# Where the modulation of both layers and the scan's step sizes run in a two-layer hybrid diffusion block

## The chip, the cores and the metric

The kernel runs on one core of a Trainium2 chip, as one program. The time is that of a whole execution on the device, in microseconds (us), median of repeated runs. The core has five engines with instruction streams of their own, each in order: TensorE (PE) for matmuls, VectorE (DVE), ScalarE (ACT), GpSimd (POOL), and SyncE (SP), which here only issues DMAs. They wait for each other by semaphores.

## What is computed

Two layers act on 1024 latent and 256 context tokens, 1024 wide, fp32. A conditioning vector for the latent tokens, another for the context, gives by a 1024 x 6144 product per layer shifts, scales and gates (the *modulation*), 12 columns of 512:

```python
x = rms_norm(...); h = modulate(x, shift, scale)      # h * (1 + scale) + shift
p = h @ w_in                                          # split into three head groups:
#  A  6 heads of latent attention (low-rank q and kv, rotary key), all keys
#  B  6 heads of bidirectional Mamba-2 scan: conv, SiLU, then
dt = softplus(dt_raw + dt_bias)                       # step sizes, (tokens, 2 directions, 6 heads)
da = -exp(a_log) * dt                                 # decays, summed within chunks of 128 tokens
#  C  4 heads of attention in a window of +-128 tokens, with a sink logit
x = x + gate * (concat(A, B, C) @ w_out)
x = x + gate * convglu(modulate(rms_norm(x)))         # w_up, conv, gate, w_down
```

Context tokens see only context tokens; in layer 2 their output is not needed. The output is a final RMSNorm of the latent tokens.

## The kernel before, in words

Activations lie feature by token. A large product is split into high and low parts and done as three PE passes (`hhi*wh`, `hlo*wh`, `hhi*wl`), so a weight tile takes ACT a rounding (`wh`) and DVE a subtraction (`wl`, L424) before PE can use it.

A layer runs thus. `w_in_ssd` (L634) projects `krdt` (rotary key and raw step sizes) and the gate z, rotates the key (`kr_rope`, L704, with DVE's L790 to L793), then makes seven columns of scan inputs `xbc`, each with a conv on DVE (L508), stored to `fmd` and, transposed, to `tmd`: the *scan columns*. Then the attention projections, with the scan (`ssd`, L803) and after it the window attention (`swa`) as side work, then six heads of latent attention. `mix` (L1494) splits the eight mixed row blocks into high and low parts; `w_out` multiplies; `ffn` has an up part with a conv and a down part (FFN-down).

PE's order is that in which the code emits it. Background generators are stepped by a model clock: each `yield g` says that its next piece comes g model us later, and `bg` (with a delay), `tick`, `drain` and `until` work through them between the foreground's matmuls. Nothing else moves a background matmul on PE. The other engines' orders come from a scheduler with priorities, and are in order when they run.

The modulation is done in two ways. `mods` (L301) gives it to PE: the conditioning is the stationary operand, four column groups at once, in two halves of 1 MB of weights a column; `mod_out` (L364) copies the result (L368), transposes it and sums. `mods_v` (L329) gives it to DVE: multiply-accumulates with the conditioning as a scalar (L352, L354), for one or two *streams* (latent, context), then transposes on PE and sums (L361). In layer 1, columns 10 and 11 go by `mods`, 4 to 9 by `mods_v`, both in the background of the scan columns. Layer 2's 12 columns go by `mods_v` in the background of layer 1's FFN-down, the first four with two streams.

In `ssd` the step sizes (from `krdt`, transposed: `pdt`), decays and their sums (`pacs`, `pacT`) come first, then the chunks of the scan. `last` (L2022), at the start of the last attention head, splits five of the eight blocks, numbers 4 and 1 with POOL; 6 and 7 follow when the side work ends, and 2 in `w_out`. The output weights are loaded once the window attention has been emitted.

Of the kernel before, what the change touches and what calls it, by code (L numbers as in the profile page):

```python
# [9 lines left out]
F32 = mybir.dt.float32  # L10
# [49 lines left out]
def _rope_tables():  # L60
# [21 lines left out]


PACE = {
    'dt': (22.0, 22.0),
    'back0': (4.0, 4.0),
    'back': (3.0, 3.0),
    'cb': (0.5, 0.5),
# [26 lines left out]
class Emit:  # L115
# [187 lines left out]
    def mods(self, l, ns, wtile, ahead, gap, etile=None):  # L303

        nc, I = self.nc, self.I
        if len(self.modT) == l:
            self.modT.append(self.C.tile([128, 6, 2, 8], F32, name=f"modT{l}"))
        todo = [(n, half) for n in ns for half in range(2)]
        ready = []

        def load():
            if todo:
                n, half = todo.pop(0)
                ws = []
                for kp in (2 * half, 2 * half + 1):
                    w = wtile([128, 2, 512])
                    self.last_w = nc.sync.dma_start(out=w, in_=I['w_mod'][l, kp * 256:(kp + 1) * 256, n * 512:(n + 1) * 512]
                                                    .rearrange("(k p) n -> p k n", p=128))
                    ws.append(w)
                ready.append(ws)  # L320

        if ahead:
            load()
        for n in ns:
            pm = None
            for half in range(2):
                load()
                yield gap
                ws = ready.pop(0)  # L329
                pm = pm or self.b("pm")  # L330
                for i in range(4):
                    self.mm(out=pm[32 * i:32 * i + 32, :], lhsT=self.st[:, half * 4 + i, :], rhs=ws[i // 2][:, i % 2, :],
                            start=(half == 0), stop=(half == 1))
            yield from self.mod_out(l, n, pm, etile or wtile)
# [465 lines left out]
        return h, lo  # L800


    def ssd(self, l, krdt, out):  # L803
        nc, c = self.nc, l == 0
        sm = self.small[l]
        es = ExitStack()
        M = PoolTags(es.enter_context(self.tc.tile_pool(name=f"M{l}", bufs=1, reuse_waits="tile")),
                     {"small": 1, "fm": 2, "tm": 3, "ab": 4, "L": 3, "xw": 2, "cb": 2, "hf": 2, "hb": 2, "z": 2, "t": 1})
        S_ = M.tile([128, 4, 120], F32, tag="small", name=self.nm("sml"))
        dt, bias_, etot, wst = [S_[:, i, :] for i in range(4)]  # L810
        S2 = self.u(shape=[128, 10, 128], name="sml2")
        dta, tot, de, t1, av, t2 = [S2[:, i, 0:120] for i in range(6)]
        acs = de
        aexp, aT = S2[:, 6, 0:12], S2[0:120, 7, :]
        triF, triB = S2[:, 8, :], S2[:, 9, :]
        self.tri(triF, 0)
        self.tri(triB, 1)
        c3 = lambda ap: ap.rearrange("p (c j) -> p c j", j=12)
# [29 lines left out]
        nc.vector.tensor_copy(c3(acs)[:, :, 0:6], c3(p1[:, 0:120])[:, :, 0:6])  # L848
        nc.vector.tensor_copy(c3(acs)[:, :, 6:12], c3(p1[:, 120:240])[:, :, 6:12])
        nc.vector.tensor_copy(tot, p1[:, 240:360])  # L850
        yield 2.0
        p2 = self.b("pacT")
        self.tr(p2[:120, 0:128], acs)
        nc.vector.tensor_copy(aT, p2[:120, 0:128])
# [7 lines left out]
        nc.scalar.activation(etot, tot, AF.Exp)  # L862
        nc.vector.tensor_mul(wst, de, dt)

        yield 2.0

        def load_tm(k):
            t = M.tile([128, 5, 128], F32, tag="tm", name=self.nm("tm"))
# [26 lines left out]
        xw = weigh(tms[0], order[0], 1)  # L895
# [484 lines left out]
    def mla_att(self, l, vt, kbuf, qh, load, maxes, Y, last):  # L1380
# [37 lines left out]
        for h in range(NH):  # L1418
            if h % 2 == 0:
                Y[h // 2] = self.u(name="ya")  # L1420
            if h == NH - 1:
                last()
            mx = maxes(h + 1) if h + 1 < NH else iter(())
            acc = self.W.tile([128, SEQ], F32, tag="wlo", name=self.nm("acc"))
            py = self.f("py")
# [9 lines left out]
            for kt in range(NCH):  # L1435
# [19 lines left out]
                next(mx, None)  # L1455
                if kt == 2 and h + 2 < NH:
                    load(h + 2)
                self.tick()
            if c:
                Pc = ctx_scores(h, terms)  # L1460
# [492 lines left out]
    def body(self):  # L1953
# [17 lines left out]
        for l in range(DEPTH):  # L1971
# [10 lines left out]
            with ExitStack() as es:  # L1982
                self.TD = PoolTags(es.enter_context(tc.tile_pool(name=f"TD{l}", bufs=1, reuse_waits="tile")), {"t": 2, "tt": 2, "wm": 6})
                if c:
                    def early():
                        wt = lambda shape, name="wm": self.TD.tile(shape, F32, tag="wm", name=self.nm(name))
                        prm = self.load_params(1, wt)
                        next(prm)
                        yield from self.mods(0, (10, 11), wt, True, 3.0)
                        next(prm, None)  # L1990
                        yield from self.mods_v(0, range(4, 10), wt, 3.7, lag=6.0)
                    self.bg(early())
                next(w_in)
                self.drain()

# [1 line left out]

            def side():
                self.scan = True
                yield from self.ssd(l, krdt, out)  # L2000
                self.scan = False
                self.bg(self.scan_norm(l, Y, out["vst"]), PACE['sn0'][l])
                yield from self.swa(l, Y)
# [6 lines left out]
                while not self.ready:  # L2010
                    yield 2.0
                for i in (6, 7):
                    self.mix(l, Y, i, hl, i in (4, 1))

            self.ready, self.paced = False, True
            self.bg(side())
# [2 lines left out]
            kbuf, qh, load, maxes = self.mla_loads(l)  # L2019
            vt = self.mla_proj(l, kva, qn, kbuf, qh, load, maxes)  # L2020

            def last():  # L2022
                self.ready = True
                for i in (3, 4, 5, 0, 1):
                    self.mix(l, Y, i, hl, i in (4, 1))

            finish = self.mla_att(l, vt, kbuf, qh, load, maxes, Y, last)
            self.drain()
# [6 lines left out]
            if l + 1 < DEPTH:  # L2035
# [7 lines left out]
                    return self.X.tile(shape, F32, tag="wm", name=self.nm("wm"))  # L2043

                def mods():
                    yield from self.mods_v(l + 1, range(12), xw, 3.8, xa, lambda n: 2 if n < 4 else 1, lag=5.0)
                    self.gated = True

                self.gated = False
                nxt = Norm(self, x, l + 1, 0, CHUNKS, CHUNKS[:2])  # L2050
                self.ffn(l, x, norm, nxt.feed, lambda: self.bg(mods(), 14.0), lambda: self.until(lambda: self.gated))
                h, need = (nxt.hi, nxt.lo), nxt.need
            else:
                feed = self.final(x)
# [182 lines left out]
```

## Time and profile before

| | us |
|---|---|
| three runs | 3250.32, 3252.76, 3253.66 (median 3252.76) |
| profiled execution | 3254.55 |
| its span on the core | 3252.8 |
| PE busy | 3052.2 (94%) |
| DVE busy | 2124.4 (65%) |
| ACT busy | 1273.7 (39%) |
| POOL busy | 597.1 (18%) |

The span counts from the first to the last instruction of the core. PE rows have modelled ends: consecutive full-width products start 0.23 us apart at the full clock, though each is shown as 0.39 long. A stretch with PE below 100% is one in which it waits.

### The profile page before, as it was taken

How to read it: one execution, taken by the hardware profiler on the slowest of the kernel's cores; microseconds unless marked ns; L12 is line 12 of the kernel's file. 1: busy time of each engine (PE TensorE's matmuls, PEld its weight loads, DVE VectorE, ACT ScalarE, POOL GpSimd, SP SyncE). 2: the span in 40 equal slices, each digit the busy share in tenths (PEclk: the TensorE clock that was granted, in tenths of full speed). 3: DMA queues.
4: the chain of work that ended last, by engine and by line, in shares of the span. 5: the costliest groups of instructions: out<-in, count | busy, mean ns of one | idle time of the engine just before them, and what ended most of it. 6: DMA issues, size and time to landing. Idle time of an engine off the chain costs nothing.

```text
span 3252.8 us, 40148 instructions
## 1 busy us (share of the span) xinstructions
PE 3052.2 (94%) x15369; PEld 2400.3 (74%) x15369; DVE 2124.4 (65%) x3134; ACT 1273.7 (39%) x2204; POOL 597.1 (18%) x375
## 2 busy tenths in 40 slices
PE   7989978998999999998999999888999999999998
PEld 4778754554878888887888788754557778888887
DVE  4784887776285665658875734788563677677544
ACT  5333543444163343443111533553342454444212
POOL 2104533443100000000000303544452000000001
PEclk9989988999999999999999999988999999999999
DMA  8765675202302212227543345655113122225321
GB/s 270 219 192 140 215 230 165 48 16 81 110 30 72 78 62 72 68 68 288 176 155 95 124 117 171 209 185 145 42 39 110 52 78 82 88 83 181 130 75 62
DMA packets 349247, 392.41 MB, mean 121 GB/s; under 512 B 37202, under 2 KB 276451, under 8 KB 349056
## 3 DMA queue, kind: packets, MB, share of 16 engines
q1 hardware_dynamic: 348092, 389.62, 38.0%
q8 instruction: 121, 1.98, 0.3%
q0 software_dynamic: 704, 0.14, 0.1%
q14 instruction: 70, 0.57, 0.1%
q10 hardware_dynamic: 260, 0.10, 0.0%
HBM read 284.48 MB, written 104.01 MB: 119 GB/s over the span
## 4 chain that ended last, share of the span: by engine, by line
PE 79%; DVE 13%; DMA 3%; ACT 2%; issue 2%; POOL 1%; SPq 0%; DVEq 0%; ACTq 0%; POOLq 0%
PE p L143 36%; PE X L143 10%; PE Z L143 7%; PE s L143 5%; PE py L143 5%; PE pc L143 4%; PE V L143 3%; PE Y L143 3%; DVE mx L1358 1%; PE pm L143 1%; PE pn L143 1%; DVE wm L354 1%; PE pst L143 1%; DMA xr<-in_x_dram 1%; DVE sh L791 1%
## 5 line engine op out<-in xcount | busy, mean ns | idle before, releaser
L143 PE MATMUL p<-gh,wb 128*128 128x512 f32 (+1 forms) x1760 | 504.9, 370 | 0.0
L436 ACT CAST wb<-w 128x512 fp32r<-128x512 f32 (+1 forms) x412 | 251.6, 613 | 599.8 <-PE p L143 308.8
L437 DVE TENSOR_TENSOR wb<-w,wb 128x512 fp32r<-128x512 f32 (+1 forms) x412 | 279.5, 680 | 237.8 <-ACT wb L436 236.6
L143 PEld LDWEIGHTS p<-gh,wb 128*128 128x128 f32 x1760 | 321.0, 189 | 55.9 <-issue 0.2
L1568 DVE SCALAR_TENSOR_TENSOR x<-p,modT,x 128x512 f32<-128x512 f32 (+1 forms) x280 | 193.5, 695 | 254.0 <-PE p L143 253.7
L143 PE MATMUL X<-hb,wb 128*128 128x512 f32 x1440 | 340.4, 389 | 1.6 <-DVE cm L1606 1.6
L143 PE MATMUL p<-gl,wb 128*128 128x512 f32 (+1 forms) x880 | 325.3, 370 | 0.3 <-DVE gl L1747 0.3
L143 PEld LDWEIGHTS X<-hb,wb 128*128 128x128 f32 x1440 | 270.1, 188 | 58.5 <-DVE cm L1606 2.5
L143 PE MATMUL p<-hhi,wh 128*128 128x512 f32 (+1 forms) x792 | 293.4, 378 | 5.5 <-ACT z L643 3.2
L143 PE MATMUL p<-hlo,wh 128*128 128x512 f32 (+3 forms) x792 | 291.3, 369 | 1.4 <-POOL hlo L2139 0.9
L143 PE MATMUL p<-hhi,wl 128*128 128x512 f32 (+1 forms) x744 | 273.5, 368 | 3.0 <-DVE wl L424 2.3
L143 PE MATMUL Z<-hb,wb 128*128 128x512 f32 x960 | 231.4, 390 | 3.8 <-ACT cm L1608 3.8
L1442 ACT ACTIVATE P<-s 128x512 f32<-128x512 f32 x240 | 142.5, 598 | 231.6 <-PE s L143 221.0
L2085 POOL TENSOR_TENSOR acc<-acc,sq 128x512 f32<-128x512 f32 x24 | 32.1, 1340 | 1024.0 <-ACT sq L2084 1024.0
L143 PEld LDWEIGHTS Z<-hb,wb 128*128 128x128 f32 x960 | 178.8, 188 | 40.9 <-ACT cm L1608 4.6
L1449 POOL TENSOR_TENSOR acc<-acc,P 128x1024 f32<-128x1024 f32 x69 | 169.5, 2457 | 197.9 <-ACT P L1442 171.8
L143 PEld LDWEIGHTS p<-gl,wb 128*128 128x128 f32 x880 | 166.7, 189 | 28.3 <-DVE gl L1747 0.8
L143 PEld LDWEIGHTS p<-hhi,wh 128*128 128x128 f32 x792 | 152.7, 194 | 34.8 <-issue 4.4
L143 PE MATMUL py<-P,vt 128*64 128x512 f32 (+3 forms) x744 | 174.5, 585 | 0.0
L143 PEld LDWEIGHTS p<-hlo,wh 128*128 128x128 f32 (+1 forms) x792 | 150.6, 190 | 25.0 <-DVE hlo L2133 1.5
L143 PEld LDWEIGHTS p<-hhi,wl 128*128 128x128 f32 x744 | 143.2, 193 | 27.4 <-DVE wl L424 3.2
L354 DVE SCALAR_TENSOR_TENSOR wm<-wm,mstat,wm 128x512 f32<-128x512 f32 x196 | 141.1, 745 | 19.9 <-DMA wm<-in_w_mod_dram 19.2
(406 smaller groups left out, 5952.9 us busy)
## 6 DMA issues: line engine op xcount, KB each, us to landing
wm<-in_w_mod_dram SPq DMA_DIRECT2D x96, 512.0 KB
w<-in_ffn_w_up_dram SPq DMA_DIRECT2D x88, 512.0 KB
w<-in_ffn_w_down_dram SPq DMA_DIRECT2D x32, 512.0 KB
w<-in_w_in_dram SPq DMA_DIRECT2D x30, 512.0 KB
gd<-ft SPq DMA_DIRECT2D x22, 640.0 KB
gr<-gd SPq DMA_DIRECT2D x22, 640.0 KB
ab<-acsd SPq DMA_DIRECT2D x36, 384.0 KB
tm<-tmd SPq DMA_DIRECT2D x38, 320.0 KB
```

What stands on the lines that cost most here:

```text
L143: self.nc.tensor.matmul(out=out, lhsT=lhsT, rhs=rhs, start=start, stop=stop, **kw)
L354: nc.vector.scalar_tensor_tensor(out=acc[:, v, :], in0=w[:, i, :], scalar=c, in1=acc[:, v, :], op0=ALU.mult, op1=ALU.add)
L436: self.nc.scalar.copy(t[:, 0], raw)
L437: self.nc.vector.tensor_sub(t[:, 1], raw, t[:, 0])
L791: nc.vector.tensor_mul(sh[:rows, LAT], sh[:rows, LAT], sin[:rows, LAT])
L1358: nc.vector.tensor_reduce(out=m[:, j, s:s + 1], in_=p, axis=AXX, op=ALU.max)
L1442: nc.scalar.activation(P[:, q * 512:(q + 1) * 512], s, AF.Exp, scale=sc)
L1449: (nc.vector if kt in ((2, 4, 6, 8) if self.scan else (4, 7)) else nc.gpsimd).tensor_add(acc, acc, P)
L1568: self.nc.vector.scalar_tensor_tensor(out=t[:, s:e], in0=p[:, 0:e - s], scalar=self.mcol(l, v, m)[:, o:o + 1], in1=t[:, s:e], op0=ALU.mult ...
L2085: (nc.gpsimd if self.n[ch] < 6 else nc.vector).tensor_add(acc, acc, sq[:, :n])
```

## The change

Layer 1's modulation columns 4 to 11 all go to PE, in one call, with the transposes of layer 2's parameters (`prm`) behind them. Layer 2's first four columns go to PE too, and start 8 instead of 14 model us into FFN-down; the other eight stay on DVE. The first part of `ssd` becomes `ssd_dt`, a background generator of its own in the scan columns, with new model times. `last` is in two parts, the second in the middle of the last head, and no `mix` uses POOL.

```diff
 PACE = {
-    'dt': (22.0, 22.0),
+    'dt': (40.0, 16.0),
+    'dt2': (12.0, 8.0),
...
     def mods(self, l, ns, wtile, ahead, gap, etile=None):
...
             self.modT.append(self.C.tile([128, 6, 2, 8], F32, name=f"modT{l}"))
+            nc.vector.memset(self.modT[l], 0.0)
...
-    def ssd(self, l, krdt, out):
+    def ssd_dt(self, l, krdt, out):
...
-        S_ = M.tile([128, 4, 120], F32, tag="small", name=self.nm("sml"))
-        dt, bias_, etot, wst = [S_[:, i, :] for i in range(4)]
-        S2 = self.u(shape=[128, 10, 128], name="sml2")
+        S_ = self.u(shape=[128, 10, 128], name="sml")
+        dt, bias_, etot, wst, dta, tot, de, t1, av, t2 = [S_[:, i, 0:120] for i in range(10)]
+        out["dt"] = dt, bias_, etot, wst
+        S2 = self.u(shape=[128, 4, 128], name="sml2")
...
         nc.vector.tensor_copy(tot, p1[:, 240:360])
-        yield 2.0
+        yield PACE['dt2'][l]
...
         nc.vector.tensor_mul(wst, de, dt)
-        yield 2.0
+    def ssd(self, l, out):
...
+        dt, bias_, etot, wst = out["dt"]
...
             if h == NH - 1:
-                last()
+                last(0)
...
+                if kt == 4 and h == NH - 1:
+                    last(1)
...
-                        yield from self.mods(0, (10, 11), wt, True, 3.0)
+                        yield from self.mods(0, range(4, 12), wt, True, 5.5)
                         next(prm, None)
-                        yield from self.mods_v(0, range(4, 10), wt, 3.7, lag=6.0)
                     self.bg(early())
+                self.bg(self.ssd_dt(l, krdt, out), 4.0)
                 next(w_in)
                 self.drain()
...
-                yield from self.ssd(l, krdt, out)
+                yield from self.ssd(l, out)
...
-                    self.mix(l, Y, i, hl, i in (4, 1))
+                    self.mix(l, Y, i, hl)
...
-            def last():
+            def last(part):
                 self.ready = True
-                for i in (3, 4, 5, 0, 1):
-                    self.mix(l, Y, i, hl, i in (4, 1))
+                for i in ((3, 4, 5), (0, 1))[part]:
+                    self.mix(l, Y, i, hl)
...
-                    yield from self.mods_v(l + 1, range(12), xw, 3.8, xa, lambda n: 2 if n < 4 else 1, lag=5.0)
+                    yield from self.mods(l + 1, range(4), xw, False, 6.0, xa)
+                    yield from self.mods_v(l + 1, range(4, 12), xw, 4.6, xa, lambda n: 1, lag=5.0)
...
-                self.ffn(l, x, norm, nxt.feed, lambda: self.bg(mods(), 14.0), lambda: self.until(lambda: self.gated))
+                self.ffn(l, x, norm, nxt.feed, lambda: self.bg(mods(), 8.0), lambda: self.until(lambda: self.gated))
```

The order on PE, at three places. Line numbers of after are shifted by one in this part of the file; numbers in names count tiles.

First, layer 1's scan columns, between the first column's last product (`p_885` before, `p_886` after) and the second column's products. Before:

```order
L143 MATMUL p_885<-hlo_582,wh_625 128x512
L143 MATMUL p_885<-hhi_581,wl_626 128x512
L143 MATMUL pm_932<-wm_909,mstat 32x512 x2
L143 MATMUL pm_932<-wm_911,mstat 32x512 x2
L143 MATMUL p_945<-hhi_396,wh_625 128x512
L143 MATMUL p_945<-hlo_397,wh_625 128x512
```

and after:

```order
L144 MATMUL p_886<-hlo_583,wh_626 128x512
L144 MATMUL p_886<-hhi_582,wl_627 128x512
L149 MATMUL pdt_937<-ident,krdt_462 128x44 x10
L144 MATMUL p_982<-hhi_397,wh_626 128x512
L144 MATMUL p_982<-hlo_398,wh_626 128x512
```

Where the first half of modulation column 10 stood (`pm`), the ten transposes of `krdt` for the step sizes (`pdt`) stand now; the modulation comes nine products later.

Second, the end of the scan columns of layer 1, from the last column's last product to the attention projections (`p_1964`, `p_1957`). Before:

```order
L143 MATMUL p_1825<-hhi_581,wl_1465 128x256
L148 MATMUL pt_1867<-ident,wm_1777 128x128 x4
L148 MATMUL pt_1873<-ident,wm_1777 128x128 x4
L148 MATMUL pt_1905<-ident,wm_1880 128x128 x4
L148 MATMUL pt_1911<-ident,wm_1880 128x128 x4
L148 MATMUL pt_1943<-ident,wm_1918 128x128 x4
L148 MATMUL pt_1949<-ident,wm_1918 128x128 x4
L143 MATMUL p_1964<-hhi_396,wh_1606 128x512
L143 MATMUL p_1964<-hlo_397,wh_1606 128x512
L143 MATMUL p_1964<-hhi_396,wl_1607 128x512
L148 MATMUL pdt_1975<-ident,krdt_461 128x44 x10
```

and after:

```order
L144 MATMUL p_1892<-hhi_582,wl_1518 128x256
L144 MATMUL pm_1922<-wm_1821,mstat 32x512 x2
L144 MATMUL pm_1922<-wm_1823,mstat 32x512 x2
L144 MATMUL pm_1922<-wm_1876,mstat 32x512 x2
L144 MATMUL pm_1922<-wm_1878,mstat 32x512 x2
L149 MATMUL pt_1933<-ident,wm_1931 128x128 x4
L149 MATMUL pa_1940<-ident,ra_897 128x98
L149 MATMUL pa_1940<-ident,rb_898 128x88
L144 MATMUL p_1957<-hhi_397,wh_1659 128x512
```

Before, six groups of modulation transposes (`pt`) and, three products on, the step sizes; now both halves of the last modulation column, its transposes, and those of the parameters (`pa`).

Third, the last group of window attention in layer 1 (`py<-P,vt` and the row sums `pd`), which before stands in the last attention head (`s_6410`, `s_6415`). Before:

```order
L143 MATMUL s_6391<-qh_5488,kl_5485 128x512
L143 MATMUL py_6170<-P_6299,vt_4372 64x384 x2
L143 MATMUL py_6170<-P_6343,vt_4372 64x384 x2
L143 MATMUL py_6170<-P_6370,vt_4372 64x256 x2
L143 MATMUL pd_6403<-acc_6169,ones 64x512 x2
L143 MATMUL s_6410<-qh_5488,kh_5484 128x512
L143 MATMUL s_6410<-ql_5489,kh_5484 128x512
L143 MATMUL s_6410<-qh_5488,kl_5485 128x512
L143 MATMUL s_6415<-qh_5488,kh_5484 128x512
L143 MATMUL s_6415<-ql_5489,kh_5484 128x512
L143 MATMUL s_6415<-qh_5488,kl_5485 128x512
L143 MATMUL pd_6421<-acc_5794,ones 64x512 x2
```

and after:

```order
L144 MATMUL s_6090<-qh_5149,kl_5146 128x512
L144 MATMUL px_6098<-kh_5522,qh_5526 128x256 x2
L144 MATMUL py_5867<-P_6006,vt_4058 64x384 x2
L144 MATMUL py_5867<-P_6030,vt_4058 64x384 x2
L144 MATMUL py_5867<-P_6068,vt_4058 64x256 x2
L144 MATMUL pd_6109<-acc_5866,ones 64x512 x2
L144 MATMUL pd_6115<-acc_5454,ones 64x512 x2
L144 MATMUL py_5954<-P_5955,vt_3666 64x512 x2
L144 MATMUL py_5954<-P_5994,vt_3666 64x512 x2
```

It now stands in the head before the last, among that head's scores (`s_6090`) and the maxima for the next (`px`), and the row sums of the head (`pd_6115`) follow at once.

## Rows read from the trace of the kernel before

**Rows 1.** Page, busy table: engine, busy us, share of the span, instructions.
```profile
PE 3052.2 (94%) x15369; PEld 2400.3 (74%) x15369; DVE 2124.4 (65%) x3134; ACT 1273.7 (39%) x2204; POOL 597.1 (18%) x375
```

**Rows 2.** Stretches: length, busy us by engine, granted clock, DMA share, GB/s.
```profile
130.00:212.00 82.00, 82.00 (x468) 71.95 (x467) 79.32 (x141) 28.82 (x46) 0.00 (x0) 1.00 0.76 237
212.00:236.00 24.00, 12.32 (x59) 9.98 (x58) 19.70 (x43) 8.82 (x11) 0.00 (x0) 0.64 0.56 173
380.00:520.00 140.00, 102.36 (x583) 73.97 (x582) 120.75 (x176) 64.88 (x148) 58.98 (x33) 0.84 0.74 237
745.00:805.00 60.00, 46.23 (x203) 26.15 (x203) 37.69 (x25) 27.78 (x41) 24.95 (x9) 0.89 0.27 86
1478.00:1560.00 82.00, 70.16 (x352) 59.53 (x352) 72.55 (x127) 22.05 (x44) 0.00 (x0) 0.94 0.75 262
1760.00:1772.00 12.00, 6.82 (x32) 5.77 (x31) 6.92 (x12) 0.90 (x2) 0.00 (x0) 0.86 0.32 67
2070.00:2235.00 165.00, 136.24 (x708) 91.21 (x708) 141.88 (x206) 78.32 (x177) 80.66 (x45) 0.87 0.72 218
```

**Rows 3.** PE's timeline, layer 1's columns: start, us, operation, [wait <-releaser].
```profile
104.93 1.06 PE L143 MATMUL pm<-wm,mstat 128*32 128x512 f32 x8
105.93 0.50 PE L143 MATMUL p<-hhi,wh 128*128 128x512 f32 x1
...
115.09 0.66 PE L148 MATMUL pt<-ident,wm 128*128 128x128 f32 x4 [2.20 <-DVE wm L368]
...
126.35 0.60 PE L148 MATMUL pt<-ident,wm 128*128 128x128 f32 x4
126.79 0.25 PE L148 MATMUL pa<-ident,ra 98*128 98x98 f32 x1
...
226.16 1.94 PE L148 MATMUL pt<-ident,wm 128*128 128x128 f32 x8 [10.91 <-DVE wm L354]
231.12 0.63 PE L143 MATMUL p<-hlo,wh 128*128 128x512 f32 x1
231.55 0.63 PE L143 MATMUL p<-hhi,wl 128*128 128x512 f32 x1
```

**Rows 4.** PE's timeline, FFN-down of layer 1, first and last of three waits.
```profile
1523.96 1.12 PE L148 MATMUL pt<-ident,wm 128*128 128x128 f32 x4 [8.55 <-DVE wm L354]
...
1766.55 1.09 PE L148 MATMUL pt<-ident,wm 128*128 128x128 f32 x4 [5.18 <-DVE wm L354]
```

**Rows 5.** PE's timeline, end of layer 1.
```profile
762.52 1.98 PE L143 MATMUL pd<-acc,ones 128*64 128x512 f32 x4 [9.43 <-DVE acc L1179]
...
795.86 0.73 PE L143 MATMUL p<-mixh,w 128*128 128x512 f32 x2 [3.98 <-DVE w L424]
```

**Rows 6.** DVE's timeline, the end of krdt's rotation, layer 1.
```profile
113.22 1.21 DVE L793 TENSOR_TENSOR krdt<-krdt,sh 32x1024 f32<-32x1024 f32 x1
```

**Rows 7.** SP's timeline, last fmd store and first tm load, layer 2.
```profile
1955.77 0.36 SPq L646 DMA_DIRECT2D fmd<-xbc  x1
1959.03 1.29 SPq L869 DMA_DIRECT2D tm<-tmd  x3
```

**Rows 8.** Chain of waits, landing of a modulation tile: start, us, what.
```profile
1755.84 3.60 DMA wm<-in_w_mod_dram
```

**Rows 9.** POOL's timeline, first weightings of the scan, layer 2.
```profile
1982.52 1.61 POOL L874 TENSOR_TENSOR xw<-tm,sml 128x384 f32<-128x384 f32 x2 [125.26 <-DVE sml L863]
```

**Rows 10.** SP's timeline, output weights of layer 1.
```profile
778.68 15.82 SPq L413 DMA_DIRECT2D w<-in_w_out_dram  x5
```

**Rows 11.** DVE's timeline, last window group's row sums, layer 1.
```profile
755.01 7.36 DVE L1179 TENSOR_TENSOR acc<-acc,P 128x768 f32<-128x768 f32 x3
```

**Rows 12.** PE's waits in 380 to 520, longest: total us, times, longest.
```profile
PE pr L143 <- DVE mr L1364: 6.8, 1, 6.8
```

**Rows 13.** Stretches in the opening of FFN-down, columns as in Rows 2.
```profile
1476.00:1484.00 8.00, 7.67 (x39) 6.19 (x38) 6.64 (x10) 0.52 (x1) 0.00 (x0) 1.00 1.03 416
1484.00:1492.00 8.00, 8.00 (x44) 6.88 (x43) 3.15 (x5) 1.24 (x3) 0.00 (x0) 1.00 1.00 362
```

More of the change, by code (lines that the diff above doesn't have):

```diff
@@ L800, in split @@
         return h, lo
-    def ssd(self, l, krdt, out):
+    def ssd_dt(self, l, krdt, out):
         nc, c = self.nc, l == 0
         sm = self.small[l]
-        es = ExitStack()
-        M = PoolTags(es.enter_context(self.tc.tile_pool(name=f"M{l}", bufs=1, reuse_waits="tile")),
-                     {"small": 1, "fm": 2, "tm": 3, "ab": 4, "L": 3, "xw": 2, "cb": 2, "hf": 2, "hb": 2, "z": 2, "t": 1})
-        S_ = M.tile([128, 4, 120], F32, tag="small", name=self.nm("sml"))
-        dt, bias_, etot, wst = [S_[:, i, :] for i in range(4)]
-        S2 = self.u(shape=[128, 10, 128], name="sml2")
-        dta, tot, de, t1, av, t2 = [S2[:, i, 0:120] for i in range(6)]
+        S_ = self.u(shape=[128, 10, 128], name="sml")
+        dt, bias_, etot, wst, dta, tot, de, t1, av, t2 = [S_[:, i, 0:120] for i in range(10)]
+        out["dt"] = dt, bias_, etot, wst
+        S2 = self.u(shape=[128, 4, 128], name="sml2")
         acs = de
-        aexp, aT = S2[:, 6, 0:12], S2[0:120, 7, :]
-        triF, triB = S2[:, 8, :], S2[:, 9, :]
+        aexp, aT = S2[:, 0, 0:12], S2[0:120, 1, :]
+        triF, triB = S2[:, 2, :], S2[:, 3, :]
         self.tri(triF, 0)
@@ L863, in ssd @@
         nc.vector.tensor_mul(wst, de, dt)
-        yield 2.0
+    def ssd(self, l, out):
+        nc, c = self.nc, l == 0
+        sm = self.small[l]
+        es = ExitStack()
+        M = PoolTags(es.enter_context(self.tc.tile_pool(name=f"M{l}", bufs=1, reuse_waits="tile")),
+                     {"fm": 2, "tm": 3, "ab": 4, "L": 3, "xw": 2, "cb": 2, "hf": 2, "hb": 2, "z": 2, "t": 1})
+        dt, bias_, etot, wst = out["dt"]
+        c3 = lambda ap: ap.rearrange("p (c j) -> p c j", j=12)
         def load_tm(k):
```

## The prediction, made before the changed kernel ran

> **What bounds the kernel now.** I read the page first: TensorE (PE) is busy 94% of the span [rows 1], so the time is PE's work plus the stretches in which it waits or runs at the lower clock. Next the table of stretches [rows 2]: PE fills 130 to 212 us completely, but only 12.3 of 24 us in 212 to 236, 102.4 of 140 in 380 to 520, 46.2 of 60 in 745 to 805, 70.2 of 82 in 1478 to 1560, and 136.2 of 165 in 2070 to 2235. These are the places where a change of order can pay. Then PE's timeline, where the bracket at a row's end is the wait before it and its releaser; there the reader is to see who is late. At the end of layer 1's scan columns it is VectorE's (DVE's) modulation sum (10.91 us) [rows 3]; three more such waits lie in FFN-down [rows 4]; at the end of layer 1 it is the window attention's row sum (9.43) and the output weights (3.98) [rows 5].
>
> **Layer 1's columns (92 to 236 us).** Columns 4 to 9 of the modulation leave DVE, and with them three waits of PE, 2.20 the first and 10.91 the last [rows 3], 13.9 us in all. After the last one PE runs at the lower clock: products start 0.43 us apart there (231.12, 231.55), twice the pace of the full clock, and the granted clock of the stretch is 0.64 [rows 2, 3]. From 226.16 to about 233 that is some 7 us of which half is lost: 3.5. Removed: 17.4.
>
> Added on PE: half a column is 8 records that take 104.93 to 105.93, with the longer first product behind it 1.1 us; a column has two, 2.2. Its four transposes take 126.35 to 126.79, 0.44; the eight of the old way fall away, 0.88 [rows 3]. Net 1.8 a column, six columns: +10.6.
>
> The scan's step sizes now start in the middle of the columns. The transposes pdt stand where PE is at 104.9 in the old trace, but they read krdt after its rotation, and the last instruction of that on DVE starts at 113.22 and takes 1.21: 114.43 [rows 6]. What is ahead of it on DVE (weight splits, a shuffle, a product) is in the same order as before, so nothing brings it forward. Behind pdt on PE stands everything: the next column's products and the modulation. So PE waits 114.43 - 104.9 = 9.5 us, and by the pattern of 226.16 loses another 3.5 at the lower clock: +13. Bounds: 0, if the wait is only the 2.20 that the first modulation column had at the same time (115.09); 16, if the conv taps queued behind it hold the PSUM buffers too. I take 13.
>
> The last column's products, its copy, four transposes and the parameters' two now come at the end without columns to hide them: 2.2 (the wait of 115.09 for just such a copy) to 4.4; I take 3. Sum of this stretch: -17.4 + 10.6 + 13 + 3 = +9.
>
> **The scan's start.** Step sizes and decays are ready early, so the first scan products follow the columns at once, and a new wait can come: their tm tiles are loaded after the last fmd store, and in layer 2 these two are 3.3 us apart on SP's queue (1955.77, 1959.03) [rows 7]. A load's landing of about 2 to 3.6 (the 512 KB of 1755.84 took 3.60 [rows 8]) and one weighting of 0.8 (the two of 1982.52 took 1.61 together [rows 9]) put the first operand at about 1963, while PE, counted by its rows, would be there at about 1956. I take +6 in layer 2 (0 to 10), +1.5 in layer 1 (0 to 4), where the drain covers most.
>
> **The end of layer 1.** The side work runs ahead: by PE's order the window attention ends before the last attention head instead of within it, and the output weights, issued at 778.68 [rows 10], behind the window attention, are early. The waits 9.43 and 3.98 [rows 5] go, and with them about 2 at the lower clock (granted 0.89 in 745 to 805 [rows 2]): 9.4 + 4 + 2 = 15.4. What is late next: the sum acc of the last window group still follows its last probabilities directly, one or two of the three additions that took 7.36 together at 755.01 [rows 11], 2.45 each; I keep 3. Net -12.5 (-15 to -4). That mix 4 and 1 now run on DVE instead of GpSimd I cost at nothing: head 5 is all score products, which cover them; without that cover the two put off a row sum by as much as one of those additions each, 4.9 in all.
>
> **The middle of each layer.** Projections, scan and attention products share 380 to 520, where PE idles 37.6 us, and 2070 to 2235, where it idles 28.8, with DVE busy 121 of 140 and 142 of 165 [rows 2]. The scan starts some 30 us earlier, so part of its DVE work leaves this stretch. What waits there are small single waits (6.8 us the longest [rows 12]), which move with any shift. I take -5 in layer 1 (-15 to +8) and -4 in layer 2 (-12 to +8).
>
> **Layer 2's modulation, in FFN-down.** Its three waits, 8.55 the first and 5.18 the last [rows 4], 16.5 in all, and about 5 us at the lower clock behind them (the granted clock is 0.94 and 0.86 in 1478 to 1560 and 1760 to 1772 [rows 2]) go: -21.5. Four columns on PE: 4 x 1.8 = +7.1; copies not ready for their transposes +2. New is that PE itself now waits for the modulation's weights, with only two x-tiles to hold them: each half column needs two loads of 512 KB, and a single one took 3.60 [rows 8], while the halves stand 35 to 42 PE rows (8 to 9.5 us) apart. From the first down-projection weight to the sixteenth half-column load, SP's order holds 28.8 MB, some 24 of them after 1478, and PE passes that part in 74 us. At the 362 GB/s of 1484 to 1492 [rows 13] they take 66 us and only the opening waits, about 3; at the mean of 262 of 1478 to 1560 [rows 2] they take 92, 18 too late. The stretch is nearer to the fuller row in its opening and to the mean later; I take +10 (3 to 20). Sum: -21.5 + 7.1 + 2 + 10 = -2.4.
>
> The windows show 416 GB/s in 1476 to 1484 and 362 in the next [rows 13]. The Trainium skill, "DMA: Bandwidth & Descriptors", section "Where 436 GB/s comes from", puts the limit of transfers between HBM and SBUF at about 358 GB/s for a core: by that the 24 MB are an estimated 67 us and the wait stays small, but no rate above 358 would be possible. The trace shows one for 8 us, so here the measurement decides.
>
> **Sum.** +9 + 1.5 + 6 - 12.5 - 5 - 4 - 2.4 = -7.4 on the profiled execution, 3254.55 - 7.4 = 3247.2. That execution is 1.8 above the median of the runs shown, 3252.76; on that basis 3245.4. A measurement of this kernel tells 0.2% (6.5 us) from no change, so the forecast lies just beyond that bound.
>
> **Rivals.**
> 1. *Slower: PE is chained to the modulation's weights in FFN-down.* Two buffers, in-order loads behind gated activations and down weights. For it: 262 GB/s is what the stretch moved at a DMA share of 0.75 [rows 2]. Against it: 362 to 416 at full share [rows 13]. Price: 18 to 20 instead of 10, and half that again at the lower clock, +14 on the forecast: 3260. It decides from the point where two loads take longer than the 8 us between halves, below about 130 GB/s for the modulation alone.
> 2. *Much faster: the earlier scan empties the middle.* For it: DVE's 86% in 380 to 520 and 2070 to 2235 [rows 2]. Against: the waits there are of several kinds, the longest 6.8 of 37.6 us [rows 2, 12]. Price -15 and -12 instead of -5 and -4: 3227.
> 3. *Nothing: the waits only move.* The end of layer 1 is won, but the scan, placed earlier, crowds the projections, and the middle costs +3 in all instead of -9: 3257; with the end of layer 1 at its larger bound, -15, and the first scan wait at none, 3249. Together about 3253.
>
> **How the numbers follow.** Forecast 0.38, rival 1 0.22, rival 2 0.20, rival 3 0.20. The forecast's own range is 3238 to 3252, of which two thirds lie below 3246.3: 0.25 faster, 0.13 same. Rival 2 is all faster, 0.20. Rival 3 is 0.14 same, 0.03 each side. Rival 1 is 0.21 slower, 0.01 same. So faster 0.48, same 0.28, slower 0.24. The range reaches from rival 2's price less its spread to rival 1's with the pdt wait at its bound of 16: 3223 to 3267.
>
> **What would show it.** Right: a PE wait of 8 to 11 us at pdt near 105, none at about 215 to 226; no 9 us wait in 745 to 805; PE waits on wm transfers instead of DVE in FFN-down. Wrong: pdt without a wait (the columns then win 4 instead of losing 9), PE waits above 15 us on wm, or the PE share in 380 to 520 and 2070 to 2235 moving by more than 10 us.

## The result: slower, and where the time went

The changed kernel takes 3281.7 us (3273.7 to 3292.7, four runs), against 3251.5 for the kernel before on the same chip: 1.0086 times as long, 95% interval 1.0068 to 1.0103. The forecast was 3245.4, with a range to 3267. The profiled execution has a span of 3272.0 us, 19.2 above that of before; it is the quickest of the four, with a mean granted clock of 0.970 against 0.960 in the slowest, so the trace shows two thirds of the loss.

TensorE is still busy 94% [rows 1], but has 13 us more work in its rows (some of it at the lower clock); DVE has 99 us less. The page's busy table of after, columns as before:

```profile
PE 3065.6 (94%) x15489; PEld 2392.7 (73%) x15489; DVE 2025.6 (62%) x2976; ACT 1277.2 (39%) x2207; POOL 587.2 (18%) x374
```

Stretches of after that answer to those of before [rows 2], moved along with the work in them except for 380 to 520, which is the same stretch. Columns as there.

```profile
130.00:212.00 82.00, 81.92 (x469) 61.55 (x468) 29.90 (x67) 31.07 (x47) 0.00 (x0) 1.00 0.74 226
212.00:246.00 34.00, 29.95 (x177) 22.65 (x177) 11.68 (x25) 9.74 (x15) 1.62 (x2) 1.00 0.67 205
380.00:520.00 140.00, 99.39 (x551) 79.37 (x552) 102.12 (x169) 56.12 (x129) 42.22 (x27) 0.83 0.78 244
745.00:815.00 70.00, 61.91 (x268) 33.67 (x265) 53.98 (x41) 32.54 (x50) 27.59 (x10) 0.93 0.18 62
1500.00:1583.00 83.00, 78.50 (x414) 57.70 (x412) 53.24 (x94) 22.45 (x45) 0.00 (x0) 0.98 0.83 299
2085.00:2260.00 175.00, 145.46 (x750) 102.95 (x749) 143.99 (x212) 77.83 (x168) 71.14 (x39) 0.84 0.66 206
```

The reader is to see three things. In 130 to 212 DVE fell from 79 to 30 us and PE gained nothing, since it was full before. In 212 to 246 the clock stays at 1.00, where it was 0.64 in 212 to 236. And 380 to 520 and 2085 to 2260, where a gain was forecast, are as idle as before or worse, at clocks of 0.83 and 0.84.

PE's timeline of after at the places of the forecast [rows 3 to 5], and at other waits that the text below needs:

```profile
111.00 1.29 PE L149 MATMUL pdt<-ident,krdt 44*128 44x44 f32 x10 [9.42 <-DVE krdt L795]
...
235.83 0.66 PE L149 MATMUL pt<-ident,wm 128*128 128x128 f32 x4 [1.41 <-DVE wm L370]
...
244.79 0.92 PE L144 MATMUL pst<-xw,tm 128*128 128x192 f32 x4 [2.64 <-POOL xw L881]
...
338.60 4.34 PE L144 MATMUL pn<-sq,ones 128*128 128x512 f32 x6 [5.79 <-DVE sq L405]
...
488.19 0.79 PE L144 MATMUL pm<-kh,qh 96*128 96x512 f32 x1 [12.37 <-DVE ql L1219]
...
747.59 1.94 PE L144 MATMUL pd<-acc,ones 128*64 128x512 f32 x8 [1.55 <-DVE acc L1186]
...
755.33 0.65 PE L144 MATMUL s<-qh,kh 97*128 97x512 f32 x1 [1.78 <-DVE acc L1400]
...
772.46 1.03 PE L144 MATMUL pd<-acc,ones 128*64 128x256 f32 x4 [3.52 <-DVE acc L1184]
...
830.44 0.66 PE L144 MATMUL p<-mixh,w 128*128 128x512 f32 x1 [4.06 <-DVE acc L1400]
...
1527.05 1.93 PE L144 MATMUL pm<-wm,mstat 128*32 128x512 f32 x8 [2.52 <-DMA wm<-in_w_mod_dram]
...
1979.57 1.65 PE L144 MATMUL pst<-xw,tm 128*128 128x192 f32 x4 [6.85 <-POOL xw L881]
```

The wait at pdt, at the first scan products (244.79 and 1979.57), and the absence of any large wait around 226 are there as forecast. So is FFN-down: instead of three waits of 16.5 us in all [rows 4] there are 2.5 on a weight transfer and 1.3 on a copy. What was not forecast are the 5.79 us in front of 338.60, the 12.37 in front of 488.19, and the 4.06 in front of 830.44, in the output projection.

The rest of the document uses one table, made from the traces: all these programs do the same main products (the matmuls into `p`, of the projections and the FFN) in the same order, so the times of the same product can be compared. *Columns*: from the 160th to the 720th main product of layer 1 (the seven scan columns and a few products on either side). *Attention*: from there to the first product of the output projection. *FFN-down*: of layer 1. *Layer 2*: from its first product to its output projection. Each is the profiled execution's difference from that of before, in us, good to some 0.3, since the cuts could stand a product earlier or later (only the changed kernel's 8.4 and 18.5 would become 11.9 and 15.1 with the cut one product later, behind the scan's first wait); the medians and ratios are those of the timed runs, each against the kernel before on the same chip.

| run | columns | attention | FFN-down | layer 2 | median | ratio (95%) |
|---|---|---|---|---|---|---|
| changed kernel | +8.4 | +18.5 | -7.1 | +9.8 | 3281.7 | 1.0086 (1.0068 to 1.0103) |
| only_ffn | -1.8 | +1.9 | -9.4 | +5.8 | 3240.9 | 0.9958 (0.9946 to 0.9971) |
| mix_ffn | -0.4 | -5.5 | -9.5 | +1.9 | 3242.5 | 0.9969 (0.9956 to 0.9981) |
| only_cols | +19.9 | +0.4 | -0.5 | +5.0 | 3271.1 | 1.0052 (1.0035 to 1.0069) |
| cols_whole | +1.4 | +7.0 | -1.3 | +3.8 | 3258.2 | 1.0012 (1.0002 to 1.0023) |
| no_dt | +17.3 | -0.6 | -8.4 | +4.8 | 3269.6 | 1.0046 (1.0032 to 1.0060) |
| only_dt | +12.1 | +18.5 | +0.6 | +11.9 | 3294.3 | 1.0119 (1.0096 to 1.0142) |
| scan_late | +7.8 | +20.5 | -7.4 | +6.5 | 3278.0 | 1.0073 (1.0051 to 1.0095) |
| swa_late | +7.7 | +12.7 | -7.4 | +11.8 | 3269.0 | 1.0044 (1.0029 to 1.0059) |
| pdt_late | +24.9 | +20.0 | -7.7 | +8.7 | 3293.5 | 1.0124 (1.0106 to 1.0142) |
| scan_mid | +28.7 | +16.8 | -9.0 | +2.3 | 3293.0 | 1.0119 (1.0101 to 1.0137) |
| scan_24 | +8.3 | +5.2 | -6.0 | +6.9 | 3264.2 | 1.0026 (1.0012 to 1.0041) |
| slot_only | -0.3 | +4.9 | -0.4 | +5.1 | 3267.0 | 1.0042 (1.0028 to 1.0056) |
| one_col | -3.0 | +2.4 | -7.3 | +11.9 | 3251.3 | 0.9999 (0.9989 to 1.0008) |

Stretches that an edit does not touch vary too: layer 2 by 4 to 5 in only_cols and cols_whole, the attention of layer 1 by +0.4 to +7.0 in only_ffn, only_cols and cols_whole. Between mix_ffn and one_col, whose order on PE is the same there, the attention differs by 8 and layer 2 by 10. So a single profile tells little below 8 to 10 us in these stretches, and the timed medians decide.

### The profile page after: what moved, and what is told of

It reads as the page before. It is cut to its first block, busy times and chain, and to the rows that moved or that the text cites. A ratio compares the mean times of both kernels' runs of the same rounds, so it can differ in the third digit from the quotient of the medians.

```text
span 3272.0 us, 40213 instructions
## 1 busy us (share of the span) xinstructions
PE 3065.6 (94%) x15489; PEld 2392.7 (73%) x15489; DVE 2025.6 (62%) x2976; ACT 1277.2 (39%) x2207; POOL 587.2 (18%) x374
## 4 chain that ended last, share of the span: by engine, by line
PE 69%; DVE 10%; DMA 2%; issue 2%; ACT 2%; POOL 1%; SPq 0%; DVEq 0%; ACTq 0%; POOLq 0%
PE p L144 28%; PE X L144 10%; PE Z L144 7%; PE s L144 5%; PE pc L144 4%; PE py L144 4%; PE V L144 3%; PE Y L144 3%; DVE mx L1365 1%; DVE acc L1400 1%; PE pm L144 1%; PE pn L144 1%; DVE hb L2173 1%; POOL acc L1456 0%; PE pd L144 0%
## 5 line engine op out<-in xcount | busy, mean ns | idle before, releaser
L1456 POOL TENSOR_TENSOR acc<-acc,P 128x1024 f32<-128x1024 f32 x72 | 179.4, 2492 | 198.2 <-ACT P L1449 156.5
L1365 DVE TENSOR_REDUCE mx<-pm 128x1 f32<-128x512 f32 x192 | 127.4, 679 | 39.0 <-PE pm L144 38.3
```

Of the source, the lines that this page charges most:

```text
L1365: nc.vector.tensor_reduce(out=m[:, j, s:s + 1], in_=p, axis=AXX, op=ALU.max)
L1456: (nc.vector if kt in ((2, 4, 6, 8) if self.scan else (4, 7)) else nc.gpsimd).tensor_add(acc, acc, P)
```

## The experiments

### First: which part loses

Theory 1 was that the scan, started early, crowds the attention projections, and pdt's wait comes on top; theory 2 that the modulation on PE and the mixes are to blame.

*no_dt*: the changed kernel, the step sizes back at the scan's start and their results back in the scan's own pool of buffers.

```diff
-                self.bg(self.ssd_dt(l, krdt, out), 4.0)
...
-                yield from self.ssd(l, out)
+                yield from self.ssd(l, krdt, out)
```

> The changed kernel with the step sizes and decays back at the scan's start, everything else of the change kept. Theory 1 (the early scan: scan and window attention, started earlier, put loads and in-order DVE and ACT chains in front of the attention projections of both layers; pdt's wait of 9.4 us comes on top): no wait at pdt, no 12 us wait at the attention projections of layer 1; 3251.5 - 4 (columns) - 7 (FFN-down) = about 3240, at most 3246. Theory 2 (the loss in layer 1's middle comes from the modulation on PE and the mixes on DVE, through changed buffers and transfers): only pdt's 13 us go, 3281.7 - 13 = about 3268, at least 3260.

Measured: 3269.6. That is theory 2's time, but not for its reason: the middle is free of loss again (-0.6), as theory 1 has it, while the columns, forecast at a gain without pdt's wait, lose 17.3. PE's waits in 90 to 265 of this run, then four rows of its timeline:

```profile
PE ptr L148 <- ACT tm L535: 10.1, 5, 2.0
PE pm L143 <- DMA wm<-in_w_mod_dram: 4.2, 2, 2.9
PE p L143 <- ACT z L644: 3.1, 1, 3.1
PE pt L148 <- DVE wm L369: 1.6, 2, 0.8
```

```profile
128.31 1.06 PE L143 MATMUL pm<-wm,mstat 128*32 128x512 f32 x8
...
133.66 1.04 PE L148 MATMUL ptr<-ident,xbc 128*128 128x128 f32 x8
...
136.73 0.44 PE L148 MATMUL ptr<-ident,xbc 128*128 128x128 f32 x2 [2.03 <-ACT tm L535]
...
139.19 1.06 PE L143 MATMUL pm<-wm,mstat 128*32 128x512 f32 x8
```

The first half of a modulation column stands at 128.31, the second at 139.19: its tile in PSUM (the memory that PE writes to), one of three in its pool, is held from one to the other. The transposes of the scan inputs (ptr) come in three groups between them, with two tiles left, and the third group has to wait until ACT has emptied the first. In after they fall behind the second half (140.20), and do not wait:

```profile
142.01 1.25 PE L149 MATMUL ptr<-ident,xbc 128*128 128x128 f32 x10
```

*only_dt*: the kernel before, with the early step sizes alone (and, as in the change, their results in the shared pool).

```diff
+                self.bg(self.ssd_dt(l, krdt, out), 4.0)
...
-                yield from self.ssd(l, krdt, out)
+                yield from self.ssd(l, out)
```

> The kernel before with the step sizes and decays moved into the scan columns, and nothing else of the change. Theory 1: pdt waits about 9.5 us, and the middle of layer 1 costs some 15, layer 2 some 3 to 10 more: about 3251.5 + 28 = 3280 (3270 to 3290). Theory 2: only pdt's wait with its lower clock, +13: about 3265, at most 3268.

Measured: 3294.3, +41, above what theory 1 said, and 18.5 in the attention of layer 1. This part alone is worse than the whole change.

*scan_late*: the changed kernel, with the scan put off.

```diff
+                yield 26.0
                 yield from self.ssd(l, out)
```

> The changed kernel with 26 model us ahead of the scan itself, so that step sizes are early and the scan's chunks and the window attention stand about where they stood before. Theory 1: the wait for xw at the scan's start goes (2.6 and 6.9 us), the 12 us wait at the attention projections goes, pdt's stays: 3281.7 - 15 - 8 = about 3258. Theory 2: the early scan is harmless, so 3275 to 3282.

Measured: 3278.0; theory 1's 3258 is missed by 20, and the time lies in theory 2's range. The 12 us wait at the projections is gone, as it said, but the attention still loses 20.5: the window attention now stands later than before, is waited for within the last head (5.41, 3.59), and its last row sums are waited for right before the output projection (3.55):

```profile
768.11 0.37 PE L144 MATMUL sr<-identr,smr 128*1 128x128 f32 x2 [5.41 <-DVE smr L1123]
...
773.46 0.37 PE L144 MATMUL sr<-identr,smr 128*1 128x128 f32 x2 [3.59 <-DVE smr L1123]
...
818.62 1.12 PE L144 MATMUL pd<-acc,ones 128*64 128x256 f32 x4 [3.55 <-DVE acc L1184]
```

*only_ffn*: the kernel before, with layer 2's columns 0 to 3 on PE.

```diff
-                    yield from self.mods_v(l + 1, range(12), xw, 3.8, xa, lambda n: 2 if n < 4 else 1, lag=5.0)
+                    yield from self.mods(l + 1, range(4), xw, False, 6.0, xa)
+                    yield from self.mods_v(l + 1, range(4, 12), xw, 4.6, xa, lambda n: 1, lag=5.0)
```

(and the start at 8 instead of 14, and the zeroing of `modT` that is in the change.)

> The kernel before with layer 2's first four modulation columns on PE, and nothing else of the change. Both theories: FFN-down of layer 1 gets 7 us shorter, as it did in the changed kernel (337 to 330 us), the rest stays: 3251.5 - 7 = about 3244.5. If part of that gain came from the other parts (less queued on DVE), 3248 to 3252.

Measured: 3240.9, faster than before by 0.42%, FFN-down -9.4. This part of the change is a gain by itself.

### Second: the columns, the window attention, the mixes

*only_cols*: the kernel before, with layer 1's columns 4 to 9 on PE.

```diff
-                        yield from self.mods(0, (10, 11), wt, True, 3.0)
+                        yield from self.mods(0, range(4, 12), wt, True, 5.5)
...
-                        yield from self.mods_v(0, range(4, 10), wt, 3.7, lag=6.0)
```

> The kernel before with layer 1's modulation columns 4 to 9 on PE and nothing else of the change. Theory 3 (formed on the run without the early step sizes): these columns are a loss by themselves, since a column's result tile is held in PSUM from its first half to its second, the transposes of the scan inputs (ptr) then wait 2.0 us for ACT in each column, weights come late at the end, and the work itself is 10 us: 3253 + 17 = about 3270, with five ptr waits of 2 us. Theory 1 unchanged (the columns are worth -4, and the loss of the run without early step sizes comes from its mixes): about 3249.

*cols_whole*: the same, with both halves of a column multiplied together.

```diff
+        if len(ns) == 8:
+            for n in ns:
+                load()
+                load()
+                yield 2 * gap
+                pm = self.b("pm")
+                for half in range(2):
...
+                yield from self.mod_out(l, n, pm, etile or wtile)
+            return
```

> As the run with only layer 1's columns on PE, but both halves of a column are multiplied together, so that its PSUM tile is held for 2 us and not for some 10. Theory 3: the ptr waits (10 us in all) go and the columns cost some 10 us less, about 3260; the wait for weights may grow, since four tiles must be there at once. If the ptr waits stay, the held tile is not their cause, and the time stays near 3270.

Measured: 3271.1 and 3258.2, both as theory 3 said. PE's waits in 88 to 275, first of only_cols, then of cols_whole:

```profile
PE ptr L148 <- ACT tm L535: 10.1, 5, 2.0
PE pm L143 <- DMA wm<-in_w_mod_dram: 4.3, 2, 3.1
PE p L143 <- ACT z L644: 3.1, 1, 3.1
PE pt L148 <- DVE wm L369: 1.6, 2, 0.8
```

```profile
PE pt L148 <- DVE wm L382: 7.6, 6, 2.0
PE pt L148 <- DVE xbc L522: 2.8, 2, 1.4
```

The ptr and weight waits go with the held tile (14.4 us), and waits for the copy come (7.6). The held tile is shown to be the cause of the ptr waits. Still the modulation on PE in these columns is no gain: 1.0012.

*swa_late*: the changed kernel, the window attention of layer 1 put off.

```diff
+                yield 12.0 if c else 0.0
                 yield from self.swa(l, Y)
```

> The changed kernel with the window attention of layer 1 started 12 model us later, everything else kept. Theory 1's second half (the 12.4 us wait at 488 us is PE behind a cast that stands in ACT's order behind the window attention's rotation, which waits for its loads): the wait falls below 4 us and the kernel gains 10 to 15, 3281.7 - 12 = about 3269. If the attention projections are short of DVE whatever stands there, the wait only changes its place: 3278 to 3284.

Measured: 3269.0, as theory 1 said for the time. What held PE in after is seen in ACT's and DVE's timelines there:

```profile
483.58 1.26 ACT L1056 CAST swh<-swr 128x1280 fp32r<-128x1280 f32 x1 [9.70 <-DVE swr L795]
484.75 1.32 ACT L1218 CAST qh<-p 64x512 fp32r<-64x512 f32 x3
```

```profile
477.52 0.01 DVE L792 LOAD_MASK_SELECT sh<-swr  x1 [3.77 <-DMA swr<-swd]
...
482.32 1.22 DVE L795 TENSOR_TENSOR swr<-swr,sh 128x1024 f32<-128x1024 f32 x1 [2.23 <-POOL swr L794]
...
487.47 0.67 DVE L1219 TENSOR_TENSOR ql<-p,qh 64x512 fp32r<-64x512 f32 x1
```

`swr` is a block of the window attention's queries or keys; its rotation waits 3.77 for its load, then for GpSimd, and ACT's rounding of it 9.70 for the rotation. The three casts `qh` of the latent attention, which PE needs, stand behind that in ACT's order. In swa_late the wait is gone, but its trace shows another of 10.0 (the scan's norm, `dg`, behind the same chain on DVE), and its profiled span is only 1.5 shorter than after's. The time agrees with the theory; the trace shows the wait moved, so the term is not settled by this run.

```profile
PE pn L144 <- DVE dg L405: 10.0, 1, 10.0
PE pn L144 <- DVE sq L405: 5.8, 1, 5.8
PE p L144 <- DVE ql L1219: 4.6, 1, 4.6
...
```

*mix_ffn*: only_ffn and the split `last`, with all mixes on DVE.

```diff
-                for i in (3, 4, 5, 0, 1):
-                    self.mix(l, Y, i, hl, i in (4, 1))
+                for i in ((3, 4, 5), (0, 1))[part]:
+                    self.mix(l, Y, i, hl)
```

> The kernel before with layer 2's first columns on PE and the mixes on DVE in two parts, without the two other parts of the change. If the mixes are harmless, as forecast: as the run with layer 2's columns alone, about 3241, or some us less, since the 9.4 us wait at the end of layer 1 has the mixes in front of its sums on DVE. If they cost: 3246 and above.

Measured: 3242.5, the mixes are harmless, as forecast; the 9.43 us wait before the window group's sums [rows 5] is 6.2 there. It and only_ffn are faster than both kernels compared here.

### Third: can the early step sizes be saved

*pdt_late*: the changed kernel, pdt put behind the key's rotation.

```diff
-                self.bg(self.ssd_dt(l, krdt, out), 4.0)
+                self.bg(self.ssd_dt(l, krdt, out), 17.0 if c else 4.0)
```

> The changed kernel with the step sizes' transposes (pdt) 13 model us later in layer 1, behind the end of the key's rotation. If the wait of 9.4 us and the lower clock behind it are an own cost, as forecast: no wait at pdt and 3281.7 - 13 = about 3268. If it only holds off the waits that the modulation columns make anyway (the run without early step sizes had five of 2.0 us at ptr in their place): 3275 to 3283.

*scan_mid*: that, and the scan put off by 12 and 8.

```diff
+                yield 12.0 if c else 8.0
                 yield from self.ssd(l, out)
```

> The changed kernel with pdt 13 model us later in layer 1 and the scan itself 12 (layer 1) and 8 (layer 2) model us later. Theory 1 (the early scan costs the middle of layer 1 some 15 us and the first scan product of layer 2 6.9): pdt's wait goes or turns into ptr's, the wait for xw in layer 2 goes, the end of layer 1 keeps its gain: about 3260 (3254 to 3266). If not the scan's start but its mere overlap with the columns costs: 3270 and above.

Measured: 3293.5 and 3293.0. pdt_late is a miss, 10 above the upper end of what was said. scan_mid misses theory 1 and lies where the overlap with the columns was to put it. The wait at pdt is gone, and PE's waits in 88 to 260 of pdt_late are these:

```profile
PE ptr L149 <- ACT tm L536: 14.4, 5, 3.5
PE pm L144 <- DMA wm<-in_w_mod_dram: 3.9, 2, 2.7
PE p L144 <- ACT z L645: 3.1, 1, 3.1
PE pt L149 <- DVE wm L370: 1.6, 2, 0.8
```

The columns lose 24.9 instead of 8.4. The place of pdt had shifted the modulation halves past the ptr groups; without it 14.4 us of ptr waits come back. pdt's wait is real, but it was in exchange for a larger one. In scan_mid the attention still loses 16.8, with the scan put off by 12; put off by 26 (scan_late) it loses 20.5. So the scan's being early is not by itself the cost.

*one_col*: mix_ffn, with only column 9 moved to PE in layer 1, before the first ptr.

```diff
-                        yield from self.mods(0, (10, 11), wt, True, 3.0)
+                        yield from self.mods(0, (9, 10, 11), wt, True, 3.0)
...
-                        yield from self.mods_v(0, range(4, 10), wt, 3.7, lag=6.0)
+                        yield from self.mods_v(0, range(4, 9), wt, 3.7, lag=6.0)
```

> The kernel before with layer 2's first columns on PE, the mixes in two parts on DVE, and of layer 1's columns only number 9 moved to PE, beside 10 and 11, early enough to end before the first ptr. Theory 3: one column less frees 12 us of DVE, so that PE's wait of 10.9 at the end of the columns and the 3.5 at the lower clock go, for 2 to 3 us of PE's work: 3242.5 - 12 = about 3231. If the wait stays whatever DVE is spared: 3243 or above.

Measured: 3251.3, a miss. The wait of 10.9 fell to 5.3 and the columns gained 3, but layer 1's attention and layer 2, whose order on PE is the same as in mix_ffn, were 8 and 10 us longer. Why is open.

### Fourth: places or buffer

*scan_24*: the changed kernel, with the scan put off so that the window attention stands where it stood before.

```diff
+                yield 24.0
                 yield from self.ssd(l, out)
```

> The changed kernel with the scan itself 24 model us later, which puts the window attention on exactly the places in TensorE's order that it had before, and the scan nearly so; step sizes stay early. Theory 1 in its first form (where scan and window attention stand decides): from the end of the columns to the output projection of layer 1 the time is that of before, 554 us, and not 573; 3281.7 - 19 = about 3262. Theory 4 (the early step sizes take a buffer of the shared pool U for the whole scan, which other tiles then wait for, wherever the scan stands): still 570 or more in that stretch, 3275 to 3282.

*slot_only*: the kernel before, with the step sizes' results in the shared pool.

```diff
-        S_ = M.tile([128, 4, 120], F32, tag="small", name=self.nm("sml"))
-        dt, bias_, etot, wst = [S_[:, i, :] for i in range(4)]
+        S_ = self.u(shape=[128, 10, 128], name="sml")
+        dt, bias_, etot, wst = [S_[:, i, 0:120] for i in range(4)]
```

(and the scan's own pool without that buffer.)

> The kernel before, with the four result tiles of the step sizes in a buffer of the shared pool U instead of one of the scan's own pool, and nothing else of the change: nothing is computed earlier. Theory 4: the scan and the window attention wait for buffers, some 10 to 18 us more between the columns and the output projection of layer 1, 3265 to 3275. Theory 1: no difference, 3253 within 5.

Measured: 3264.2 and 3267.0. With the places restored (on PE the order from the columns to the output projection is that of before, but for the step sizes' own matmuls and three products), the attention of layer 1 loses 5.2 instead of 18.5, close to theory 1, and the median is 17.5 lower. With the buffer alone the timed ratio, 1.0042, is clear of 1, as theory 4 said; but the stretch that it took to be 10 to 18 longer is 4.9 longer. Both effects exist. By these profiles 13.3 of the 18.5 are the places; the remaining 5 agree with the buffer, though a single profile can hardly tell 5.

How the buffer acts is seen on ACT. Here are GpSimd's square sum `sq` and ACT's copy `sw` in before, then the copy in slot_only and in after:

```profile
305.66 2.95 POOL L758 TENSOR_TENSOR sq<-sq,sq 128x1280 f32<-128x1280 f32 x1 [8.56 <-ACT sq L756]
305.74 0.58 ACT L632 COPY sw<-p 128x512 f32<-128x512 f32 x1
```

```profile
305.51 0.58 ACT L632 COPY sw<-p 128x512 f32<-128x512 f32 x1 [2.79 <-POOL sq L758]
```

```profile
325.25 0.59 ACT L634 COPY sw<-p 128x512 f32<-128x512 f32 x1 [6.33 <-POOL sq L760]
```

The copy reads only `p`, PE's product, and in before it runs beside the square sum. So its wait for `sq` is one for a buffer that the sum still uses. It shows in seven of the eight runs with the results in the shared pool (all but scan_mid), with 2.8 to 6.3 us, and in none of the seven others. Behind the copy ACT has scan work and the norm's `rr`, and DVE's `sq` needs that; so PE gets a wait that it did not have, 5.79 in after (338.60 above; GpSimd also starts the sum later there, behind scan work) and this in slot_only (285 to 330):

```profile
PE pn L143 <- DVE sq L403: 2.2, 1, 2.2
```

That wait is 2.2 of the 4.9; for the rest no single wait stands out. How the timed 12.7 of this run divides over the program is open.

## Why the prediction was wrong, by its own steps

**The middle of each layer, and the end of layer 1: the steps that failed.** From the columns to the output projection of layer 1 the sum had +1.5 (scan's start), -12.5 (end) and -5 (middle), together -16; measured +18.5. The first scan product waits 2.64, near the 1.5.

At the end the waits of 9.4 and 4.0 went, as said, but 1.55, 1.78, 3.52 and 4.06 came, 10.9 for 13.4, where the sum kept 3: counted by waits a gain of some 2.5, where the sum had 12.5. (The 4.0 and the 4.06 lie just behind the stretch and cancel.) The last of them was not thought of. The last head's row sums leave PE at 822.75, but DVE takes their reciprocal only after a weight split that waits for ACT; in before it follows them within 0.2 us, at 805.25.

```profile
825.89 1.23 DVE L426 TENSOR_TENSOR wl<-w,wh 128x1024 fp32r<-128x1024 f32 x1 [3.57 <-ACT wh L425]
827.03 3.35 DVE L1400 RECIPROCAL acc<-pd 128x512 f32<-128x512 f32 x1
```

The middle was the larger error. The text took it that scan work moved ahead leaves room behind it, and bounded the loss at 8. In truth the window attention came with it, and its loads, rotation and roundings landed among the latent attention's casts, in order on ACT and DVE. That the places cost some 13 us is shown by scan_24; that the chain on ACT is all of it is not. Nor is it a matter of earlier or later: 12, 24 and 26 model us of delay leave 16.8, 5.2 and 20.5. I had read the waits of that stretch as small and of several kinds [rows 12], and did not ask what is queued behind the moved loads on ACT. The third rival named the crowding, but not what crowds, and priced the middle at +3. The forecast's signs of being wrong did not show either: PE's share in 380 to 520 and 2070 to 2235 moved by some 3 us only, so these windows were the wrong place to look for the loss.

**A buffer was not counted.** The text spoke of reordering only; the results of the step sizes now hold a buffer of a pool that other stages share. slot_only prices that at 12.7 us in the timed runs, some 5 of it in layer 1's attention by the profile, where ACT's copy waits for a buffer.

**Layer 1's columns: right sum, wrong terms.** Forecast +9, measured +8.4. But the modulation alone was forecast to gain 4 (-17.4 + 10.6 + 3) and costs 19.9, for the held PSUM tile and late weights; and pdt was forecast to cost 13, and with it the columns lose less than without, +8.4 against +17.3 (no_dt) and +19.9 (only_cols). The wait itself, 9.42, was forecast at 9.5; what it displaces was not seen. Two errors cancelled.

**FFN-down: right mechanism, mis-sized.** Forecast -2.4, measured -7.1 (-9.4 alone). The term for weight waits, +10, measured 2.8, at its low bound of 3. The transfers ran at 396, 376 and 389 GB/s in the stretches 1500 to 1524, above the row of 362 that gave that bound. The Trainium skill, "DMA: Bandwidth & Descriptors", section "Where 436 GB/s comes from", states about 358 as the limit for transfers between HBM and SBUF; the trace does not agree, also if its DMA shares of 1.01 to 1.06 mean that it counts a few per cent too much.

```profile
1492.00:1500.00 8.00, 8.00 (x37) 6.64 (x36) 6.08 (x12) 5.44 (x13) 0.00 (x0) 1.00 1.03 415
1500.00:1508.00 8.00, 7.67 (x39) 6.19 (x38) 6.33 (x10) 0.41 (x1) 0.00 (x0) 1.00 1.03 396
1508.00:1516.00 8.00, 7.92 (x43) 6.57 (x43) 3.52 (x6) 2.38 (x5) 0.00 (x0) 1.00 1.01 376
1516.00:1524.00 8.00, 7.69 (x40) 5.34 (x37) 4.98 (x10) 0.75 (x2) 0.00 (x0) 1.00 1.06 389
```

**Layer 2.** The first scan product waits 6.85, forecast 6. The middle was forecast at -4; the stretch to the output projection shows +9.8. one_col, without the early step sizes, shows +11.9, so what the change costs there is open.

**Rivals.** The slower rival, PE chained to the modulation's weights, did not happen: its waits were 2.8, not 18 to 20. No rival named the window attention or the buffer. Added up, the profile's +19.2 is +8.4 + 18.5 - 7.1 + 9.8, less 3.4 before the columns and 7.1 after layer 2's attention, both parts that the change does not touch. Why the timed median lies some 11 further above the profiled execution is open.

## What to carry to other kernels

When background work is moved ahead, follow all that comes after it in the same background: the stage behind it lands somewhere new, and what its loads and its in-order partners on the quiet engines then delay can cost more than its matmuls gain. Count the buffers that the moved results hold, too. Before adding work in pieces to a full engine, count the buffers held between the pieces. A wait seen in a trace may be what keeps a larger one away, so take it out by an experiment, not by subtraction; and part a bundle of changes, since one part here (layer 2's columns on PE) was worth 0.4% alone.

## What was not expected of the hardware

Transfers ran at 376 to 415 GB/s for 32 us on end here (1492 to 1524), where the kernel before showed such rates for 24 us at the same place (389 in the row below, then 416 and 362 [rows 13]); how much further it goes was not tried.

```profile
1468.00:1476.00 8.00, 8.00 (x37) 6.64 (x36) 5.97 (x11) 5.80 (x13) 0.00 (x0) 1.00 1.00 389
```
